# A squared-ReLU MLP in which the left half of the down projection takes seven block products for eight

## The chip, the cores and the metric

The kernel runs on one core of a Trainium2 chip. The metric is the device time of one launch, in microseconds. A core has five engines that run their own instruction queues in order and wait for each other by semaphores: TensorE (PE, matrix products into PSUM), ScalarE (ACT), VectorE (DVE), GpSimd (POOL) and SyncE (SP). In this kernel SP issues the weight loads, POOL a few small transfers, and the transfers themselves run on the core's DMA engines. PSUM has eight banks of 128 partitions by 512 float32.

## The reference

Two layers of a decoder trunk over 256 rows of 2048 columns, all in float32. Each layer is a mixer (attention of 8 heads beside a gated short convolution, one projection before and one after) and an MLP with 8192 hidden columns:

```
for l in range(DEPTH):                       # 2
    h = _rmsnorm(x, attn_norm_g[l])
    proj = h @ w_in[l]                       # 2048 x 6144: q, k, v, gate_b, gate_c, conv_in
    ...                                      # differential attention, gated causal convolution
    x = x + concat([attn, conv]) @ w_out[l]  # 2048 x 2048
    hm = _rmsnorm(x, mlp_norm_g[l]) @ w_up[l]          # 2048 x 8192
    x = x + square(relu(hm)) @ w_down[l]               # 8192 x 2048
```

## The kernel before, in words

A float32 matrix product is made of three products of halves. Each operand is split into a high part, which is the value rounded to the type that PE reads (`float32r`), and a low part, the rest; the terms are high by high, high by low and low by high (`TERMS`). Weights are loaded by SP in tiles of 512 KB (`raw`, four buffers), and each tile is split by ACT (high, L307) and DVE (low, L308) into one of three buffers, 128 by 1024 each.

There are two forms of product. `linear` (L322 to L339) holds activations still and streams 512 columns of weights: for each 128 rows of weights and each half of the 256 rows of x it issues three matmuls of 512 columns into a tile of two PSUM banks. It is used for q, k, v, o and the down projection (`dn`). `linear_t` (L341 to L364) holds 128 by 128 of weights still and streams activations, so that the result is transposed: a matmul of 512 columns does high by high and high by low at once (both parts of the activations lie side by side), and one of 256 columns does the third term. It is used for `up` and for the convolution's inputs. The two tiles of two banks that these products alternate between are called `mm`; three more banks serve transposes and small products, and one the attention's `av`.

The MLP runs in four groups of 2048 hidden columns (L650 to L666). A group first makes eight chunks of `up`, each relu'd, squared and split into `hid` tiles in SBUF, and then four products `dn`, one for each 512 columns of the output, each added onto x by two multiply-adds of DVE with the squared row scale `r2` (L659). In the last group of layer 0 each finished 512 columns of x start a `chunk` of the next normalisation (L395 on): eight transposes on PE, four splits of 128 by 256 by ACT (L244) and DVE (L245) into the next layer's `nT`, and two sums of squares on ACT (L409).

The order on PE is that of the program as written. Attention, normalisation and other small work is written as generators that a background list advances at every `tick` between matmuls. One global `plan` lists all weight tiles of both layers in order of use, and the splits run `AHEAD` = 2 tiles ahead of the product that uses them, over all borders of stages and layers. The other engines' queues get the order that the framework's scheduler chooses. The relative bias of the attention (2 MB in SBUF) is built once at the start: two transfers of 1 MB on POOL's queue out of a small table in DRAM (L208), and eight copies on ACT (L237); it stays in SBUF for both layers.

Of the kernel before, what the change touches and what calls it, by code (L numbers as in the profile page):

```python
# [9 lines left out]
F32 = mybir.dt.float32  # L10
# [22 lines left out]
AHEAD = 2  # L33
# [65 lines left out]
def trunk(ctx: ExitStack, tc: tile.TileContext, x, w_in, w_out, conv_w, q_norm_g, k_norm_g,  # L99
# [7 lines left out]
    bpool = ctx.enter_context(tc.tile_pool(name="bpool", bufs=8))  # L107
    wpool = ctx.enter_context(tc.tile_pool(name="wpool", bufs=3))
    nat = ctx.enter_context(tc.tile_pool(name="nat", bufs=7))
    tmp = ctx.enter_context(tc.tile_pool(name="tmp", bufs=3))  # L110
# [77 lines left out]
    bias = const.tile([P, 2 * NH, S], F32, tag="bias", name="bias")  # L188
# [6 lines left out]
    def small_setup():  # L195


# [4 lines left out]
        by_dist_d = dram.tile([2 * NH, REL], F32, name="by_dist_d")  # L202
        nc.gpsimd.dma_start(by_dist_d, by_dist)
        revs = []
        for j in range(2):
            rev = bpool.tile([P, NH, S], F32, tag="b", name=f"rev{j}")
            src = by_dist_d[j * NH:(j + 1) * NH, 0:S]
            nc.gpsimd.dma_start(  # L208
                rev, bass.AP(src.tensor, src.offset, [[1, P], [REL, NH], [1, S]]))
            revs.append(rev)  # L210
# [22 lines left out]

        yield 4
# [25 lines left out]

    def straight(w, row0, nk, col):
        return [(w, row0 + 2 * P * i, col, 2) for i in range(nk // 2)]

    def turned(w, col):
        return [(w, 4 * P * i, col, 4) for i in range(D // P // 4)]

    plan = []
    for l in range(DEPTH):  # L270
        for half in range(2):
            for part in range(3):
                plan += straight(w_in[l], 0, D // P, part * AW + half * CH)
        for q in range(AW // WC):
            for part in (4, 5):
                plan += turned(w_in[l], part * AW + q * WC)
        for q in range(AW // WC):
            plan += turned(w_in[l], 3 * AW + q * WC)
        for n in range(D // CH):
            plan += straight(w_out[l], 0, D // P, n * CH)  # L280
        for g in range(DFF // D):
            for c in range(D // WC):
                plan += turned(w_up[l], g * D + c * WC)
            for n in range(D // CH):
                plan += straight(w_down[l], g * D, D // P, n * CH)
    loaded, parts_of = [], []

    def load_weights():
        i = len(loaded)
        if i < len(plan):  # L290
            w, row, c, nk = plan[i]
            cols = 2 * CH // nk
            raw = wpool.tile([P, nk, cols], F32, tag="raw", name=f"raw{i}", bufs=RAW)
            nc.sync.dma_start(
                raw, w[row:row + nk * P, c:c + cols].rearrange("(k p) c -> p k c", p=P))
            loaded.append(raw)

    def split_weights():
        i = len(parts_of)
        if i < len(plan):  # L300
            while len(loaded) <= i:
                load_weights()
            nk = plan[i][3]
            hi = wpool.tile([P, nk, 2 * CH // nk], F32R, tag="hi", name=f"whi{i}")
            lo = wpool.tile([P, nk, 2 * CH // nk], F32R, tag="lo", name=f"wlo{i}")
            for c in (slice(0, 1), slice(1, nk)) if i < 2 else (slice(0, nk),):
                nc.scalar.activation(hi[:, c], loaded[i][:, c], AF.Copy)  # L307
                nc.vector.tensor_sub(lo[:, c], loaded[i][:, c], hi[:, c].bitcast(F32))  # L308
            parts_of.append((hi, lo))

    used = [0]

    def weights(w, row, c):

        i = used[0]
        used[0] += 1
        assert plan[i][1:3] == (row, c)
        while len(parts_of) < min(len(plan), i + 1 + AHEAD):
            split_weights()
        return parts_of[i]  # L320

    def linear(name, acts, w, row0, col0):  # L322

        acc = mm.tile([P, NT, CH], F32, tag="mm2", name=name)
        nk = len(acts) * KG
        for kp in range(nk // 2):
            hi, lo = weights(w, row0 + kp * 2 * P, col0)
            for j in range(2):
                k = kp * 2 + j
                a = acts[k // KG]  # L330
                while not a.ready:
                    work.tick()
                for t in range(NT):
                    for n, (pa, pw) in enumerate(TERMS):
                        nc.tensor.matmul(  # L335
                            acc[:, t], a.ap[:, pa, k % KG, t * P:(t + 1) * P], (hi, lo)[pw][:, j],
                            start=(k == 0 and n == 0), stop=(k == nk - 1 and n == 2))
                work.tick()
        return acc  # L339

    def linear_t(name, acts, w, col0):  # L341
# [6 lines left out]
        for k0 in range(0, nk, 4):  # L348
            hi, lo = weights(w, k0 * P, col0)
# [32 lines left out]
    class Norm:  # L382
# [31 lines left out]
        def factors(self):  # L414
# [8 lines left out]
            if self.which:  # L423
                self.r2 = small.tile([P, NT], F32, tag="rowf2", name="rowf2", bufs=2)
                nc.vector.tensor_mul(self.r2, self.r, self.r)
# [47 lines left out]
    def attention(l, qT, kT, v, h0, dst):  # L473
# [111 lines left out]
    def hidden(acc, dst, j, name):  # L585

        a = joined(acc, name)
        sq = nat.tile([P, 2, S], F32, tag="wide", name=f"{name}s")
        nc.scalar.activation(a, a, AF.Relu)
        nc.scalar.activation(sq, a, AF.Square)  # L590
        in_parts(dst, j, sq)


    norm = Norm(0, 0)
    work.start(norm.chunk(0, 0))
    for n in range(1, D // CH):
        load_weights()
        load_weights()
        load_x(n)
        work.start(norm.chunk(n, 2), 4 * n - 3)  # L600
    work.start(small_setup(), 10)

    for l in range(DEPTH):
        hT = norm.tiles
        cat = [Parts(bpool, "b", f"cat{l}{i}") for i in range(4)]
        work.start(norm.factors(), 1)
        for half in range(2):
            h0 = 4 * half
            c0 = half * CH
            acc = linear(f"q{l}{half}", hT, w_in[l], 0, c0)  # L610
            r = norm.r
            qT = bpool.tile([P, 2, 4, S], F32R, tag="b", name=f"qT{l}{half}")
            work.start(qk_norm(acc, r, qT, q_gain[:, l:l + 1], f"q{l}{half}"))
            acc = linear(f"k{l}{half}", hT, w_in[l], 0, AW + c0)
            kT = bpool.tile([P, 2, 4, S], F32R, tag="b", name=f"kT{l}{half}")
            work.start(qk_norm(acc, r, kT, k_gain[:, l:l + 1], f"k{l}{half}"))
            acc = linear(f"v{l}{half}", hT, w_in[l], 0, 2 * AW + c0)
            v = bpool.tile([P, 2, NT, CH], F32R, tag="b", name=f"v{l}{half}")
            for t in range(NT):
                nc.scalar.activation(v[:, 0, t], acc[:, t], AF.Copy, scale=r[:, t:t + 1])  # L620
                nc.vector.scalar_tensor_tensor(v[:, 1, t], acc[:, t], r[:, t:t + 1],
                                               v[:, 0, t].bitcast(F32),
                                               op0=ALU.mult, op1=ALU.subtract)
            work.start(attention(l, qT, kT, v, h0, cat[half]), 3)
        cv = bpool.tile([P, AW // P, S], F32, tag="b", name=f"cv{l}")
        for q in range(AW // WC):
            acc = linear_t(f"gc{l}{q}", hT, w_in[l], 4 * AW + q * WC)
            u = joined(acc, f"gc{l}{q}")
            nc.gpsimd.tensor_tensor(u, u, norm.bc(2), op=ALU.mult)
            acc = linear_t(f"ci{l}{q}", hT, w_in[l], 5 * AW + q * WC)  # L630
            i = joined(acc, f"ci{l}{q}")
            nc.vector.tensor_mul(u, i, u)
            conv(l, q, u, cv, norm)
        for q in range(AW // WC):
            acc = linear_t(f"gb{l}{q}", hT, w_in[l], 3 * AW + q * WC)
            gate(q, acc, cv, cat[2 + q // 2])

        norm = Norm(1, l)
        for n in range(D // CH):
            acc = linear(f"o{l}{n}", cat, w_out[l], 0, n * CH)  # L640
            for t in range(NT):
                nc.vector.tensor_add(xs[n][:, t], acc[:, t], xs[n][:, t])
            work.start(norm.chunk(n, 2))

        mT = norm.tiles
        G = D // CH
        last = l == DEPTH - 1
        mnorm, norm = norm, None if last else Norm(0, l + 1)
        work.start(mnorm.factors(), 1)
        for g in range(DFF // (G * CH)):  # L650
            hid = [Parts(bpool, "b", f"hid{l}{g}{c}") for c in range(G)]
            for c in range(2 * G):
                acc = linear_t(f"up{l}{g}{c}", mT, w_up[l], g * D + c * WC)
                hidden(acc, hid[c // 2], c % 2, f"h{l}{g}{c}")
            final = g == DFF // (G * CH) - 1
# [42 lines left out]
```

## Time and profile before

| | |
|---|---|
| three runs, median (lowest to highest) | 2207.14 us (2206.47 to 2209.34) |
| the profiled execution, its own time | 2209.4 us |
| its span | 2207.6 us |
| mean granted clock of PE | 0.999 |
| busy: PE, DVE, ACT, POOL | 2193.6, 1257.4, 1105.3, 100.3 us |
| moved by DMA | 410.99 MB, mean 186 GB/s |
| the MLPs in the chain, start to end | 405.9 to 1112.5 and 1499.0 to 2202.9 us |

The span is the time between the first and the last instruction of the profile; the execution's own time has 1.8 us more around it. A row of the groups view gives line, engine, operation, output and inputs, shape and count, then the busy time and the mean of one in ns, then the engine's idle time before such instructions with what ended it. A row of the windows view gives the stretch, the busy time of PE, weight load, DVE, ACT and POOL with the number of instructions, then the granted clock, the DMA engines' busy share and the bytes moved. In the chain, a piece is start, duration, what ran, and how many instructions.

### The profile page before, as it was taken

The numbers are of one execution on the slowest core, as the hardware profiler recorded it, in microseconds if no ns is written. First come the engines' busy times: TensorE is split into PE (matmuls) and PEld (weight loads), VectorE is DVE, ScalarE is ACT, GpSimd is POOL, SyncE is SP. The second block draws the span as 40 slices with busy tenths as digits, with TensorE's granted clock in tenths as the row PEclk, the third lists the DMA queues.
The fourth block names the chain that finished last, engine by engine and source line by source line (L and its number), as shares of the span: only waits on it lengthen the run. The fifth ranks groups of instructions, "written<-read, shape, count | busy, mean of one in ns | idle before, by whom it ended". The sixth has DMA issues, their size and how long they took to land.

```text
span 2207.6 us, 28973 instructions
## 1 busy us (share of the span) xinstructions
PE 2193.6 (99%) x11242; PEld 1863.1 (84%) x11242; DVE 1257.4 (57%) x1561; ACT 1105.3 (50%) x1492; POOL 100.3 (5%) x120
## 2 busy tenths in 40 slices
PE   8999999999999999999999999999999999999999
PEld 6888888888888888888888888888888888888887
DVE  5577655555555555555556776555555555555554
ACT  6456445554454454355445664445534544544543
POOL 3021100000000000000011211000000000000000
PEclk9999999999999999999999999999999999999999
DMA  7554666666666666666666546666666666666665
GB/s 250 172 158 148 191 183 189 187 187 191 197 186 188 199 187 186 194 194 184 186 185 179 156 153 187 186 185 189 188 191 196 187 190 197 185 189 199 186 197 162
DMA packets 302698, 410.99 MB, mean 186 GB/s; under 512 B 12931, under 2 KB 193749, under 8 KB 302560
## 3 DMA queue, kind: packets, MB, share of 16 engines
q1 hardware_dynamic: 301520, 406.90, 61.0%
q0 software_dynamic: 992, 2.22, 0.3%
q8 instruction: 88, 1.44, 0.3%
q14 instruction: 50, 0.41, 0.1%
q10 hardware_dynamic: 48, 0.02, 0.0%
HBM read 406.96 MB, written 2.12 MB: 185 GB/s over the span
## 4 chain that ended last, share of the span: by engine, by line
PE 99%; DMA 0%; POOL 0%; DVE 0%; ACT 0%; issue 0%; SPq 0%; DVEq 0%
PE up L357 32%; PE dn L335 32%; PE o L335 8%; PE q L335 4%; PE gc L357 4%; PE ci L357 4%; PE gb L357 4%; PE k L335 4%; PE v L335 4%; PE sc L487 1%; PE av L523 1%; PE tpn L399 1%; DMA raw<-in_w_in_dram 0%; PE ptp L513 0%; PE atp L549 0%; POOL q_r L379 0%
## 5 line engine op out<-in xcount | busy, mean ns | idle before, releaser
L308 DVE TENSOR_TENSOR wlo<-raw,whi 128x1024 fp32r<-128x1024 f32 (+1 forms) x770 | 944.0, 1226 | 835.1 <-ACT whi L307 831.5
L307 ACT ACTIVATE whi<-raw 128x1024 fp32r<-128x1024 f32 (+1 forms) x770 | 813.3, 1056 | 991.9 <-PE dn L335 387.8
L335 PE MATMUL dn<-whi,hid 128*128 128x512 f32 x2048 | 632.7, 389 | 0.0
L357 PE MATMUL up<-nT,whi 128*128 128x512 f32 x2048 | 512.6, 392 | 0.0
L335 PEld LDWEIGHTS dn<-whi,hid 128*128 128x128 f32 x2048 | 384.4, 188 | 79.6
L357 PEld LDWEIGHTS up<-nT,whi 128*128 128x128 f32 x2048 | 368.8, 189 | 66.3
L335 PE MATMUL dn<-wlo,hid 128*128 128x512 f32 x1024 | 398.5, 389 | 0.0
L357 PEld LDWEIGHTS up<-nT,wlo 128*128 128x128 f32 x2048 | 279.3, 190 | 19.8
L357 PE MATMUL up<-nT,wlo 128*128 128x256 f32 x2048 | 285.7, 282 | 0.0
L335 PEld LDWEIGHTS dn<-wlo,hid 128*128 128x128 f32 x1024 | 192.2, 188 | 39.5
L335 PE MATMUL o<-whi,cat 128*128 128x512 f32 x512 | 159.6, 390 | 0.0
L335 PEld LDWEIGHTS o<-whi,cat 128*128 128x128 f32 x512 | 96.1, 188 | 19.8
L335 PE MATMUL o<-wlo,cat 128*128 128x512 f32 x256 | 99.6, 389 | 0.0
L335 PE MATMUL q<-whi,nT 128*128 128x512 f32 x256 | 86.0, 405 | 2.8 <-ACT nT L244 2.8
L335 PE MATMUL k<-whi,nT 128*128 128x512 f32 x256 | 86.6, 405 | 0.0
L335 PE MATMUL v<-whi,nT 128*128 128x512 f32 x256 | 83.4, 396 | 0.0
L357 PE MATMUL gc<-nT,whi 128*128 128x512 f32 x256 | 65.8, 396 | 0.0
L357 PE MATMUL ci<-nT,whi 128*128 128x512 f32 x256 | 65.3, 396 | 0.0
L357 PE MATMUL gb<-nT,whi 128*128 128x512 f32 x256 | 64.1, 392 | 0.0
L335 PEld LDWEIGHTS q<-whi,nT 128*128 128x128 f32 x256 | 48.9, 191 | 14.6 <-ACT nT L244 3.2
L335 PEld LDWEIGHTS k<-whi,nT 128*128 128x128 f32 x256 | 48.9, 191 | 11.0
L335 PEld LDWEIGHTS o<-wlo,cat 128*128 128x128 f32 x256 | 48.1, 188 | 9.7
(645 smaller groups left out, 1580.5 us busy)
## 6 DMA issues: line engine op xcount, KB each, us to landing
raw<-in_w_up_dram SPq DMA_DIRECT2D x256, 512.0 KB, 3.7
raw<-in_w_down_dram SPq DMA_DIRECT2D x256, 512.0 KB, 3.7
raw<-in_w_in_dram SPq DMA_DIRECT2D x192, 512.0 KB, 4.0
raw<-in_w_out_dram SPq DMA_DIRECT2D x64, 512.0 KB, 3.7
rev<-by_dist_d POOLq DMA_DIRECT2D x2, 1024.0 KB, 11.6
out_dram<-x SPq DMA_DIRECT2D x8, 256.0 KB, 3.9
x<-in_x_dram SPq DMA_DIRECT2D x3, 512.0 KB, 9.5
x<-in_x_dram SPq DMA_DIRECT2D x2, 256.0 KB, 3.8
```

Of the source, the lines that this page charges most:

```text
L307: nc.scalar.activation(hi[:, c], loaded[i][:, c], AF.Copy)
L308: nc.vector.tensor_sub(lo[:, c], loaded[i][:, c], hi[:, c].bitcast(F32))
L335: nc.tensor.matmul(acc[:, t], a.ap[:, pa, k % KG, t * P:(t + 1) * P], (hi, lo)[pw][:, j], start=(k == 0 and n == 0), stop=(k == nk - 1 and ...
L357: nc.tensor.matmul(acc[:, f, 0] if part else acc[:, f], wt[:, k % 4, fs], a.ap[:, 0, k % KG] if part else a.ap[:, :, k % KG], start=(part ...
L399: nc.tensor.transpose(tp[:, i * S + t * P:i * S + (t + 1) * P], xs[n][:, t, k * P:(k + 1) * P], ident)
L487: nc.tensor.matmul(sc[:, :W], qT[m * DK:(m + 1) * DK, a, i, t * P:(t + 1) * P], kT[m * DK:(m + 1) * DK, b, i, :W], start=(n == 0), stop=(n ...
L523: nc.tensor.matmul(av[:, i * P:(i + 1) * P], pT[:, a, k * P:(k + 1) * P], v[:, b, k, i * P:(i + 1) * P], start=(k == 0 and n == 0), stop=( ...
```

## The change

The left 1024 of the 2048 output columns of the down projection are computed with seven block products for eight. Blocks are: two neighbouring runs of 128 hidden rows (a *pair* of hidden blocks, 32 pairs per layer), two halves of 128 rows of x, and two halves of 512 output columns. For each pair the weights need four sums (t1 to t4) and the activations four sums (S1 to S4), and the seven products of all 32 pairs stay in seven PSUM banks until the end of the stage, where eleven operations of DVE and one of ACT combine them onto x (L854 to L872 of the new file). The eighth bank takes the up columns.

The new `mlp` (L666) therefore runs by pairs. In each of 32 steps two `up_column`s of 128 hidden columns (32 matmuls each, L767) alternate with the 21 matmuls of the pair two steps earlier (`LAG`). `evict` (L788) copies the bank by ACT and adds the two halves by DVE. `square` (L793) does relu, a factor for the upper half of the rows, square, sends the hidden values to DRAM by POOL (256 KB), makes S1 to S4 on DVE and splits all eight blocks into `f`. `quarters` (L711) makes the weight forms: b1 and b2 are split directly from the loaded 1 MB tile `draw`; t1 and t3 come from a copy times minus one on ACT (L724) onto which a transfer of POOL's queue adds 512 KB of w_down out of DRAM (L725); t2 and t4 are an add and a subtract on DVE. When all pairs are through, the right 1024 columns run as before with 24 matmuls per pair, with the hidden values loaded back from DRAM (L886) and split again.

Round this: every stage has its own `Weights` list, so that splits no longer run ahead over a border; `AHEAD` is 3; the mixer's bias, temporary and raw-weight pools and `bpool` are opened inside `mixer` (L598 on) and the MLP's pools inside `mlp`, over the same SBUF; the bias is built anew for the second layer (`load_bias`, L226); the rows' scale is folded into a factor on half of the rows and one scale at the end. In layer 0 the next normalisation's chunks 0 and 1 start after the combining and chunks 2 and 3 after the last product.

```diff
-AHEAD = 2
+AHEAD = 3
+NP = DFF // (2 * P)
+LAG = 2
...
+            def parts(src, tag, bufs):
+                hi = spool.tile(list(src.shape), F32R, tag=f"{tag}h", name=f"{tag}h", bufs=bufs)
+                lo = spool.tile(list(src.shape), F32R, tag=f"{tag}l", name=f"{tag}l", bufs=bufs)
+                nc.scalar.activation(hi, src, AF.Copy)
+                nc.vector.tensor_sub(lo, src, hi.bitcast(F32))
+                return hi, lo
+            def quarters(i):
+                def plain():
+                    raw = forms["raw"] = load_rows(i, 0).rearrange("p k (n c) -> p k n c", n=2)
+                    h1, l1 = parts(raw[:, 0, 0], "b1", 2)
+                    h2, l2 = parts(raw[:, 1], "b2", 1)
+                    return (h1, l1), (h2[:, 0], l2[:, 0]), (h2[:, 1], l2[:, 1])
+                def sums():
+                    raw = forms["raw"]
+                    t = forms["t"] = spool.tile([P, 4, CH], F32, tag="t", name="t", bufs=2)
+                    nc.scalar.activation(t[:, 0:2], raw[:, 0], AF.Copy, scale=-1.0)
+                    nc.gpsimd.dma_start(
+                        t[:, 0:2], w_down[l][i * 2 * P:(i + 1) * 2 * P, CH:2 * CH].rearrange(
+                            "(k p) c -> p k c", p=P), accum_op=ALU.add)
+                    h, lw = parts(t[:, 0:2], "t13", 1)
+                    nc.vector.tensor_add(t[:, 2], t[:, 1], raw[:, 0, 0])
+                    nc.vector.tensor_sub(t[:, 3], raw[:, 1, 0], t[:, 2])
+                    return (h[:, 0], lw[:, 0]), (h[:, 1], lw[:, 1])
...
+            for i in range(NP + LAG):
+                j = i - LAG
+                if i < NP:
+                    h = fpool.tile([P, 8, P], F32, tag="h", name="h", bufs=1)
+                    evict(up_column(f"up{l}{i}a", i < LAG),
+                          h[:, 0:2].rearrange("p a c -> p (a c)"))
...
+                if j >= 0:
+                    b11, b21, b22 = weights.take()
+                    t1, t3 = weights.take()
+                    product(0, j, A11, b11)
+                    product(1, j, A12, b21)
+                    product(2, j, S4, b22)
+                    product(4, j, S1, t1)
+                if i < NP:
+                    evict(up_column(f"up{l}{i}b", i < LAG),
+                          h[:, 2:4].rearrange("p a c -> p (a c)"))
+                    fs[i] = square(i, h)
+                if j >= 0:
+                    t2, t4 = weights.take()
+                    product(6, j, S3, t3)
+                    product(5, j, S2, t2)
+                    product(3, j, A22, t4)
+            e1 = wide("e1")
+            nc.scalar.activation(e1, p1, AF.Copy, scale=mnorm.scale)
+            onto(xs[0][:, 0], p2, xs[0][:, 0])
...
+            for i in range(NP):
+                back = nat.tile([P, 2, S], F32, tag="wide", name="back")
+                nc.sync.dma_start(back.rearrange("p k s -> p (k s)"), hid[i])
+                f = fpool.tile([P, 2, 2, S], F32R, tag="f", name="fr")
+                nc.scalar.activation(f[:, 0], back, AF.Copy)
+                nc.vector.tensor_sub(f[:, 1], back, f[:, 0].bitcast(F32))
```

More of the change, by code (lines that the diff above doesn't have):

```diff
@@ L232, in small_setup, with load_bias @@
         nc.vector.tensor_copy(nlam, lps[:, :DEPTH])
+    def load_bias(l, bpool, bias):
+        if l == 0:
+            yield from small_setup()
+        revs = []
+        for j in range(2):
+            rev = bpool.tile([P, NH, S], F32, tag="b", name=f"rev{l}{j}")
+            src = by_dist_d[j * NH:(j + 1) * NH, 0:S]
+            nc.gpsimd.dma_start(
+                rev, bass.AP(src.tensor, src.offset, [[1, P], [REL, NH], [1, S]]))
+            revs.append(rev)
         yield 4
@@ L603, in trunk @@
[L603 to L655, printed above, removed]
-            for n in range(D // CH):
-                acc = linear(f"dn{l}{g}{n}", hid, w_down[l], g * G * CH, n * CH)
-                for t in range(NT):
-                    nc.vector.scalar_tensor_tensor(
-                        xs[n][:, t], acc[:, t], mnorm.r2[:, t:t + 1], xs[n][:, t],
-                        op0=ALU.mult, op1=ALU.add)
-                    if final and last:
@@ L663, in trunk @@
                         nc.sync.dma_start(
                             out[0, t * P:(t + 1) * P, n * CH:(n + 1) * CH], xs[n][:, t])
-                if final and not last:
-                    work.start(norm.chunk(n, 2))
+            else:
+                work.start(norm.chunk(0, 2), 12)
+                work.start(norm.chunk(1, 2), 24)
+            acc = [mm.tile([P, NT, CH], F32, tag="mm2", name=f"dn{l}{n}") for n in range(2)]
+            for i in range(NP):
+                back = nat.tile([P, 2, S], F32, tag="wide", name="back")
[3 more added lines that the diff above has]
+                nc.vector.tensor_sub(f[:, 1], back, f[:, 0].bitcast(F32))
+                for k in range(2):
+                    b = weights.take()
+                    for n in range(2):
+                        for t in range(NT):
+                            for m, (pa, pw) in enumerate(TERMS):
+                                nc.tensor.matmul(
+                                    acc[n][:, t], f[:, pa, k, t * P:(t + 1) * P], b[pw][:, n],
+                                    start=(i == 0 and k == 0 and m == 0),
+                                    stop=(i == NP - 1 and k == 1 and m == 2))
+                        work.tick()
@@ new lines, in mlp, with first_loads @@
+            for n in range(2):
+                for t in range(NT):
+                    onto(xs[2 + n][:, t], acc[n][:, t], xs[2 + n][:, t])
+                    if last:
+                        nc.sync.dma_start(
+                            out[0, t * P:(t + 1) * P, (2 + n) * CH:(3 + n) * CH],
+                            xs[2 + n][:, t])
+                if not last:
+                    work.start(norm.chunk(2 + n, 2))
+        return norm
+    norm = Norm(0, 0)
+    def first_loads(weights):
+        for n in range(1, D // CH):
+            weights.load_early(2)
+            load_x(n)
+            work.start(norm.chunk(n, 2), 4 * n - 3)
@@ L667, in trunk @@
+    work.start(norm.chunk(0, 0))
+    for l in range(DEPTH):
+        mnorm = mixer(l, norm, first_loads if l == 0 else lambda weights: None)
+        norm = mlp(l, mnorm, l == DEPTH - 1)
     work.finish()
```

329 lines of the change are left out of this document (247 added, 82 removed).

## The prediction

> **What bounds the kernel now.** I read the busy table and the slices first, then the chain that ended last, then the stage windows, then the groups by line, the transfers and the one early stall. The page:
>
> ```profile
> PE 2193.6 (99%) x11242; PEld 1863.1 (84%) x11242; DVE 1257.4 (57%) x1561; ACT 1105.3 (50%) x1492; POOL 100.3 (5%) x120
> PEclk9999999999999999999999999999999999999999
> ```
>
> The chain, two of its pieces, and the windows of the same two stages (a group of up, a group of dn; after the busy times come PEclk, DMA share, GB/s):
>
> ```profile
> 580.51 89.36 PE up L357 x512
> 669.87 87.07 PE dn L335 x384
> ...
> 580.51:669.87 89.36, 89.36 (x513) 78.66 (x513) 49.57 (x48) 50.03 (x61) 0.00 (x0) 1.00 0.63 189
> 669.87:756.93 87.06, 87.06 (x385) 72.07 (x385) 44.42 (x40) 35.31 (x36) 0.00 (x0) 1.00 0.63 193
> ```
>
> PE never waits: the MLP is matmuls end to end at full clock, DVE is busy for 55% and 51% of the stages, the DMA engines for 63%. So any matmul removed is time, as long as nothing else comes late. One dn matmul (512 columns) takes 87.07/384 = 0.2267 us. An up group is half such matmuls, half of 256 columns: (89.36 - 256 x 0.2267)/256 = 0.1223 us.
>
> **What is removed.** Seven products for eight on the left half is 21 matmuls in place of 24 for each of 32 pairs of 128 hidden rows, in 2 layers: 192 x 0.2267 = **43.5 us**, 0.68 us per pair. The up product and the right half keep their matmuls. A pair of up and left half lasts 32 up matmuls (5.585 us) twice and 21 x 0.2267 = 4.76: 15.93 us for 16.61 before.
>
> **What the other engines carry per pair.** Prices:
>
> ```profile
> L307 ACT ACTIVATE whi<-raw 128x1024 fp32r<-128x1024 f32 x766 | 811.0, 1059 | 986.7 <-PE dn L335 387.8 <-PE up L357 302.2 <-PE o L335 83.5
> L369 ACT ACTIVATE gb0l<-gb 128x512 f32<-128x512 f32 x2 | 1.2, 586 | 0.0
> L409 ACT ACTIVATE junk<-x 128x512 f32<-128x512 f32 x32 | 19.7, 617 | 0.0
> ```
>
> ```profile
> L308 DVE TENSOR_TENSOR wlo<-raw,whi 128x1024 fp32r<-128x1024 f32 x766 | 941.5, 1229 | 830.9 <-ACT whi L307 827.3 <-PE up L357 2.4
> L659 DVE SCALAR_TENSOR_TENSOR x<-dn,rowf,x 128x512 f32<-128x512 f32 x64 | 45.1, 747 | 18.3 <-PE dn L335 18.3
> L642 DVE TENSOR_TENSOR x<-o,x 128x512 f32<-128x512 f32 x16 | 10.3, 686 | 3.2 <-PE o L335 3.2
> L516 DVE TENSOR_TENSOR pT<-ptp,pT 128x256 fp32r<-128x256 f32 x16 | 6.7, 417 | 0.2
> L516 DVE TENSOR_TENSOR pT<-ptp,pT 128x128 fp32r<-128x128 f32 x16 | 4.5, 279 | 0.0
> ```
>
> ACT: nine 1024s (four up splits, b2, t copy, t13, t24, f), three 512s (b1, relu, square), two evictions: 9 x 1.059 + 3 x 0.617 + 2 x 0.586 = 12.6 us of 15.93. DVE: eight 1024s, three 512s (b1, two for t2 and t4), three 256s, four 128s: 8 x 1.229 + 3 x 0.686 + 3 x 0.417 + 4 x 0.279 = 14.3 us, 90%. Both fit, DVE barely; rows of single instructions count their overlap twice, so this is its upper end. The before kernel's cover (half of DVE idle) is mostly spent.
>
> **The steady pairs.** The tight place is the single bank of the up columns. Column b's first matmul may start after column a (5.585) and twelve product matmuls (2.72), 8.30 us into the pair. ACT's queue ahead of that bank's eviction is the next column's split (from 5.6), the f copy, then the eviction. The rows below show a 1024 free ACT 0.97 us after its start, so the eviction ends at 5.6 + 0.97 + 0.97 + 0.59 = 8.13. It holds, by 0.17 us; I take 0 and keep 0.1 to 0.3 us in 60 pairs (6 to 18 us) as a rival.
>
> ```profile
> 1112.54 1.06 ACT L307 ACTIVATE whi<-raw 128x1024 fp32r<-128x1024 f32 x1 [1.66 <-PE dn L335]
> ...
> 1113.51 0.61 ACT L409 ACTIVATE junk<-x 128x512 f32<-128x512 f32 x1
> ```
>
> The accumulating transfer (512 KB on POOL's queue, behind the 256 KB store of the hidden rows) has no row. From its issue, t's add on DVE and the t13 split are due some 7.8 us later, and PE itself 8.7. Nearest rows:
>
> ```profile
> raw<-in_w_up_dram SPq DMA_DIRECT2D x256, 512.0 KB, 3.7
> rev<-by_dist_d POOLq DMA_DIRECT2D x2, 1024.0 KB, 11.6
> out_dram<-x SPq DMA_DIRECT2D x8, 256.0 KB, 3.9
> ```
>
> ```profile
> 29.29 1.81 POOL L208 DMA_DIRECT2D rev<-by_dist_d  x2 [1.66 <-DMA by_dist_d<-by_dist]
> ```
>
> A plain 512 KB load plus POOL's issue is 3.7 + 0.9 = 4.6 us; the 1 MB POOL transfer took 11.6. I take 6.5, nearer the load, the same bytes in long rows: free. At 11.6 it costs 2.9 us in each of 60 pairs, 174 us. Bytes: 2 MB of up, 1 of down, 0.5 accumulated, 0.25 stored per pair is 3.93e6 bytes / 15.93 us = 247 GB/s (280 if the accumulate reads its destination), against a peak of
>
> ```profile
> 10.00:12.00 2.00, 2.00 (x7) 1.52 (x6) 2.00 (x6) 2.00 (x7) 0.95 (x2) 1.00 1.05 397
> 35.00:40.00 5.00, 5.00 (x24) 4.12 (x23) 3.06 (x7) 2.92 (x4) 0.97 (x3) 1.00 1.01 355
> ```
>
> which it fits. The Trainium skill's "DMA: Bandwidth & Descriptors", section "Anatomy of one DMA — SWDGE (gpsimd) path", gives 2.0 us + bytes/436e3 for a POOL transfer, an estimate of 3.2 us here; its "Rules for kernel authors" say that an accumulate reads its destination and writes it later, so one might count the bytes twice, 4.4 us; no run here shows either, and by both the steady pairs stay free as in my sum. They speak against the slow-transfer rival; the 11.6 us row speaks for it.
>
> **The serial places.** The old kernel crossed every stage with weights already split. After this change each stage has pools of its own over the same memory, and the queues drain. Going through each engine's order by hand, with the rows above:
>
> (a) Start of each MLP. The first 1 MB of w_down overlays a pool that the last o matmul still reads, so it is issued only after that; 3.7 us for 512 KB and another 512 KB at some 370 GB/s is 5.1 us. The b1 split of it stands in ACT's queue ahead of the second half of the last normalised chunk, which PE needs for its first column. PE waits about 4.2 us (3 to 6). Twice: 8.4. The first pairs' ramp: 0.5.
>
> (b) Drain of the last two pairs. After the last up column PE has 30 matmuls (6.8 us) before it needs f(31). In front of f(31) on ACT stand: eviction, t13, two right-half splits, relu, t24, b2 (6.5 us to here), then t13, square, t24 and one more right-half split, whose 1 MB load reuses the buffer that b2's low half (1.2) frees: 6.5 + 1.2 + 5.1 = 12.8, split and f copy 2 x 1.06, low half 1.23: about 16.2 against 6.8. Late 9.5 us (7 to 11). Twice: 19. The load is issued from SP in order; behind it wait the next right-half loads, which nobody needs yet.
>
> (c) Combining. After the last product DVE does six multiply-adds and three adds before the first right-half f can get its low half: 6 x 0.747 + 3 x 0.686 = 6.5, less the overlap back to back; PE waits 5.5 (4.5 to 7). Twice: 11. The reload of hidden rows behind it is covered by this. Before, the 64 multiply-adds stood beside matmuls.
>
> (d) Layer boundary. The next layer's q waits for the banks that the last multiply-adds read, and chunks 2 and 3, started together, need four transposing banks of three, whose splits stand behind a weight split. Before, the chunks came one dn product apart, and the same place shows no wait:
>
> ```profile
> 1112.51 2.73 PE q L335 x12
> 1115.23 0.88 PE tpn L399 x8
> 1116.11 6.84 PE q L335 x30
> ```
>
> 1.0 + 3.5 = 4.5 us (1 to 7). Second reload of the bias: eight ACT copies late, 1.5 (0 to 3). The end of the kernel and the right half itself: 0 (24 matmuls = 5.44 us per pair against 1.31e6 bytes, 241 GB/s, and three splits).
>
> (e) The clock. The only real stall of the old trace, and what followed:
>
> ```profile
> 50.65 0.40 PE L335 MATMUL k<-whi,nT 128*128 128x512 f32 x1
> 53.41 0.66 PE L465 MATMUL q00tp<-ident,q00n 128*128 128x128 f32 x4 [2.37 <-DVE q00n L456]
> ```
>
> ```profile
> 54.00:55.00 1.00, 1.00 (x5) 0.82 (x4) 1.00 (x2) 0.69 (x1) 0.00 (x0) 0.72 0.29 104
> 55.00:56.00 1.00, 1.00 (x3) 0.73 (x3) 0.81 (x2) 0.00 (x0) 0.00 (x0) 0.50 0.46 63
> 56.00:57.00 1.00, 1.00 (x4) 0.80 (x3) 0.00 (x0) 0.75 (x1) 0.00 (x0) 0.50 0.79 260
> 57.00:58.00 1.00, 1.00 (x4) 0.79 (x3) 0.66 (x1) 0.31 (x1) 0.00 (x0) 0.57 0.53 203
> 58.00:60.00 2.00, 2.00 (x10) 1.62 (x9) 0.56 (x1) 0.16 (x1) 0.00 (x0) 1.00 0.26 26
> ```
>
> 2.37 us without work cost 0.28 + 0.50 + 0.50 + 0.43 = 1.7 us of clock afterwards. Seven stalls above that length: 12 us (4 to 16). The Trainium skill, "TensorE: Matmul & The Clock Gate", Part 1, says that the rate halves after an idle window of about 3.4 us and comes back after as long a busy one. The trace agrees with the way back (0.50 for some 3.3 us) and not with the threshold, since 2.37 us sufficed. By the page, (d)'s two short waits and those of (a) in part would be spared, some 5 us less in the sum.
>
> **Sum.** 8.4 + 0.5 + 19 + 11 + 4.5 + 1.5 + 12 = 57 us of cost (34 to 75 by the ends) against 43.5 saved: +13.4 us on the profiled execution's 2209.4, which lies 2.3 above the median of 2207.14; so 2222.8, or about **2220 us** in the terms of the median, slower by 0.6%. By the ends alone 2198 to 2239.
>
> **Rivals.**
> 1. The gain is kept. The stages' matmuls go and the serial places cost 10 to 20 us: for this the drain's f(31) must come in time, so that (b) falls from 19 to a few us. For it: PE 99% of a chain with nothing else in it. Against it: the order in ACT's queue. 2207 - 43.5 + 10 to 25: 2172 to 2190. It decides where the waits together stay below 43.5 us.
> 2. The accumulating transfer is too slow. Price (L - 8.7) x 60: 10 us gives +78, 2300; 11.6 gives 2395. Decides from L = 8.7. For it the rev row, against it the 512 KB rows.
> 3. The bank's 0.17 us doesn't hold, or DVE at 90% becomes the bound: 0.1 to 0.3 us each pair, 2226 to 2240, up to 2260 with long waits.
> 4. The clock stays up in the stalls, (e) falls away: 2208, next to no change. For it: nothing in this trace; against it: the 0.50 rows after a stall shorter than most of these.
>
> **Chances.** Forecast with its own range 2198 to 2239: 0.50; rival 1: 0.20; rival 2: 0.13; rival 3: 0.12; rival 4: 0.05. A measurement of this kernel tells about 0.2% (4.4 us) from no change. Faster: rival 1 and the forecast's low end, 0.24; within: 0.13; slower: 0.63. The range 2185 to 2285 leaves out most of rival 1 and of rival 2.
>
> **What would show it.** Right: in the new trace PE busy falls by about 43 us, the steady pairs are 15.9 us with no idle PE, and the idle of PE stands at six places, behind f(31), behind fr's low half, behind the first b1 split's load, and at the second layer's first q. Accumulating transfers land within 7.8 us. Wrong: PE idle spread evenly over the pairs (rival 2 if DVE waits for the transfer, rival 3 if PE waits for the eviction), or six places of 1 us (rival 1).

## The result

| | median of the runs (lowest to highest) |
|---|---|
| the kernel before | 2208.24 us (2206.47 to 2209.40) |
| the changed kernel | 2422.47 us (2413.23 to 2425.18) |
| ratio | 1.0962, 95% interval 1.0937 to 1.0986 |

The changed kernel is 9.6% slower; the prediction said 0.6% slower (2220 us) and gave 2185 to 2285 as its range. The direction was right and the size was not: the time lies 202 us above the forecast and 137 us above the top of the range.

The page of the changed kernel, busy times and the rows of its slices for the clock (span 2418.2 us):

```profile
PE 2240.0 (93%) x11054; PEld 1875.2 (78%) x11054; DVE 1556.7 (64%) x2239; ACT 1340.5 (55%) x1822; POOL 209.7 (9%) x250
PEclk9999999999999999899999999999999999998999
...
uraw<-in_w_up_dram SPq DMA_DIRECT2D x128, 1024.0 KB, 6.9
draw<-in_w_down_dram SPq DMA_DIRECT2D x128, 1024.0 KB, 5.5
t<-in_w_down_dram POOLq DMA_DIRECT2D x64, 512.0 KB, 10.7
```

PE has fewer matmuls (11054 for 11242) and is yet busy for longer: its mean granted clock is 0.962, where it was 0.999. It is idle for 178 us where it was idle for 14. The accumulating transfer takes 10.7 us to land (the median of 64). Who waits for it stands in the view of waits (waiting instruction, what it waited for, total us, times, longest):

```profile
DVE t L730 <- DMA t<-in_w_down_dram: 345.8, 62, 8.2
ACT h L797 <- DVE h L791: 233.7, 55, 6.7
```

One pair in the trace, first DVE's queue, then POOL's issue of the transfer it waits for, then ACT's queue behind DVE, then PE in this pair and its two neighbours (start, duration, instruction, idle time before it):

```profile
709.37 1.22 DVE L708 TENSOR_TENSOR b2l<-draw,b2h 128x1024 fp32r<-128x1024 f32 x1
717.90 0.69 DVE L730 TENSOR_TENSOR t<-t,draw 128x512 f32<-128x512 f32 x1 [7.31 <-DMA t<-in_w_down_dram]
718.51 1.22 DVE L693 TENSOR_TENSOR ulo<-uraw,uhi 128x1024 fp32r<-128x1024 f32 x1
...
721.39 0.42 DVE L791 TENSOR_TENSOR h<-ev 128x256 f32<-128x256 f32 x1
```

```profile
705.47 1.20 POOL L725 DMA_DIRECT2D t<-in_w_down_dram  x1 [1.32 <-ACT t L724]
```

```profile
721.84 0.63 ACT L797 ACTIVATE h<-h 128x512 f32<-128x512 f32 x1 [6.53 <-DVE h L791]
...
727.68 0.58 ACT L790 ACTIVATE ev<-up017a 128x512 f32<-128x512 f32 x1
```

```profile
688.19 3.78 PE L779 MATMUL up015b<-nT,uhi 128*128 128x512 f32 x8 [4.00 <-ACT ev L790]
710.56 2.00 PE L779 MATMUL up016b<-nT,uhi 128*128 128x512 f32 x8
728.31 3.78 PE L779 MATMUL up017b<-nT,uhi 128*128 128x512 f32 x8 [4.42 <-ACT ev L790]
```

The transfer is issued at 705.47, and the add that waits for it starts at 717.90, 12.4 us later. This reader, the add for t2, is the next thing in DVE's queue at 710.6, five microseconds after the issue. Behind the add stand the up weights' low halves and the sum of the evicted column, so relu, square, S1 to S4 and the split into f come late, ACT's queue comes late behind them, and with it the eviction of the one bank that the up columns share. PE waits there (52 waits for this eviction in the timeline, 120 us in all, up to 4.7 us each). In the rows shown it then runs at about half rate: eight matmuls of 512 columns take 3.78 us after such a wait and 2.00 without. After 29 of the 52 waits the first eight take 2.58 us or more.

The sum itself is not needed so early. Counted in order from the start of the layer, the transfer issued at 705.47 and the add at 717.90 are the 17th of their kind, and the 17th splits of t1 and t3 and of t2 and t4 on ACT are these:

```profile
737.48 1.06 ACT L707 ACTIVATE t13h<-t 128x1024 fp32r<-128x1024 f32 x1
...
741.34 1.05 ACT L707 ACTIVATE t24h<-t 128x1024 fp32r<-128x1024 f32 x1
```

So the scheduler has put the copy, the transfer and the add a whole pair ahead of the splits (t has two buffers): the split of t1 and t3 comes 32 us after the issue, and that of t2 and t4 23 us after the add. DVE stands still for sums that are split only a pair later.

### The profile page after: what moved, and what is told of

Its sections match the earlier page's. It is cut to its first block, busy times and chain, and to the rows that moved or that the text cites. A ratio compares the mean times of both kernels' runs of the same rounds, so it can differ in the third digit from the quotient of the medians.

```text
span 2418.2 us, 29438 instructions
## 1 busy us (share of the span) xinstructions
PE 2240.0 (93%) x11054; PEld 1875.2 (78%) x11054; DVE 1556.7 (64%) x2239; ACT 1340.5 (55%) x1822; POOL 209.7 (9%) x250
## 4 chain that ended last, share of the span: by engine, by line
PE 49%; issue 39%; DMA 5%; POOL 4%; DVE 2%; ACT 2%; POOLq 0%; SPq 0%; DVEq 0%; ACTq 0%
PE dn L895 15%; PE o L337 7%; PE gc L359 4%; PE ci L359 4%; PE q L337 4%; PE gb L359 4%; PE v L337 4%; PE k L337 3%; DMA t<-in_w_down_dram 3%; POOL t L725 3%; PE pr L818 1%; POOL hid L802 1%; DMA draw<-in_w_down_dram 1%; DMA hid<-h 1%; PE sc L499 1%
## 5 line engine op out<-in xcount | busy, mean ns | idle before, releaser
L282 DVE TENSOR_TENSOR wlo<-raw,whi 128x1024 fp32r<-128x1024 f32 (+1 forms) x258 | 317.3, 1231 | 242.8 <-ACT whi L281 241.5
L281 ACT ACTIVATE whi<-raw 128x1024 fp32r<-128x1024 f32 (+1 forms) x258 | 271.3, 1053 | 310.6 <-PE o L337 73.6
L692 ACT ACTIVATE uhi<-uraw 128x1024 fp32r<-128x1024 f32 x256 | 269.4, 1052 | 219.1 <-PE o L337 10.0
L693 DVE TENSOR_TENSOR ulo<-uraw,uhi 128x1024 fp32r<-128x1024 f32 x256 | 312.2, 1221 | 29.3 <-ACT uhi L692 25.4
L895 PE MATMUL dn<-whi,fr 128*128 128x512 f32 x1024 | 320.3, 393 | 9.8 <-ACT fr L888 8.1
L282 DVE TENSOR_TENSOR wlo<-draw,whi 128x1024 fp32r<-128x1024 f32 x128 | 156.7, 1226 | 155.0 <-ACT whi L281 155.0
L895 PEld LDWEIGHTS dn<-whi,fr 128*128 128x128 f32 x1024 | 194.4, 190 | 51.8 <-ACT fr L888 8.9
L281 ACT ACTIVATE whi<-draw 128x1024 fp32r<-128x1024 f32 x128 | 135.6, 1061 | 178.2 <-PE dn L895 171.1
L895 PE MATMUL dn<-wlo,fr 128*128 128x512 f32 x512 | 200.9, 392 | 0.0
L818 PE MATMUL pr<-t13h,f 128*128 128x512 f32 x256 | 100.3, 394 | 0.0
L725 POOL DMA_DIRECT2D t<-in_w_down_dram x64 | 77.1, 1205 | 138.2 <-ACT t L724 136.0
## 6 DMA issues: line engine op xcount, KB each, us to landing
t<-in_w_down_dram POOLq DMA_DIRECT2D x64, 512.0 KB, 10.7
```

The costliest lines, as they stand in the source:

```text
L281: nc.scalar.activation(hi[:, k], raw[:, k], AF.Copy)
L282: nc.vector.tensor_sub(lo[:, k], raw[:, k], hi[:, k].bitcast(F32))
L692: nc.scalar.activation(hi, src, AF.Copy)
L693: nc.vector.tensor_sub(lo, src, hi.bitcast(F32))
L725: nc.gpsimd.dma_start(t[:, 0:2], w_down[l][i * 2 * P:(i + 1) * 2 * P, CH:2 * CH].rearrange("(k p) c -> p k c", p=P), accum_op=ALU.add)
L818: nc.tensor.matmul(prods[n], f[:, pa, a], b[pw], start=(i == 0 and m == 0), stop=(i == NP - 1 and m == 2))
```

## The experiments

Every time is the median of the runs beside the kernel before on the same chip (2208.1 to 2209.1 us); the intervals are of the ratio to it.

**e1 and e2: the transfer without the add.**

```diff
-nc.gpsimd.dma_start(t[:, 0:2], w_down[...], accum_op=ALU.add)
+nc.gpsimd.dma_start(t[:, 0:2], w_down[...])      # e1
+nc.sync.dma_start(t[:, 0:2], w_down[...])        # e2
```

> The transfer of 512 KB onto t is issued from POOL at the same place, after the same copy, but overwrites t instead of being added to it (the sum is left out, so t1 to t4 are not the sums they should be). In the changed kernel it took 10.7 us to land, and 62 of 64 times DVE waited for it, 345.8 us in all. Theory A, that adding in flight is what makes it slow: it lands in 4.6 to 6.5 us, DVE's wait falls under 60 us, the kernel takes 2422 - 200 = about 2220 us. Theory B, that any transfer of POOL's queue is slow beside the 1 MB loads: still 9 us or more, about 2420 us. Theory C, that the pairs are long for another reason (DVE's load, the one bank of the up columns): the transfer lands early and the time still stays above 2350 us.

> The same plain transfer (sum left out), issued from SP. Theory A: as e1, about 2220 us. Theory B: 4 to 5.5 us to land where e1 had 9 or more, about 2220 us, and e1 stays at 2420. If SP's queue is in the way (the transfer waits for t's copy on ACT, and the next up and down loads stand behind it), the loads come later and PE waits at the splits: 2230 to 2300 us under both.

e1 took 2221.63 us (1.0043 to 1.0073), e2 2219.13 (1.0033 to 1.0066). In e1's page, then e2's:

```profile
t<-in_w_down_dram POOLq DMA_DIRECT2D x64, 512.0 KB, 7.1
```

```profile
t<-in_w_down_dram SPq DMA_DIRECT2D x64, 512.0 KB, 5.1
```

The same bytes at the same place in the program take 10.7 us added, 7.1 us plain from POOL and 5.1 us plain from SP. Theory A had 4.6 to 6.5 us and under 60 us of DVE's waiting for e1; it is 7.1 us, and DVE still waits 78.7 us in all, but PE no longer waits in the steady pairs. So theory A holds in the main: without the add the transfer is early enough, and what lay above some 2220 us is gone. Theory B falls with e1.

**e3 and e4: the sum without a transfer.** The loaded 1 MB tile holds all four operands of t1 and t3.

```diff
-nc.scalar.activation(t[:, 0:2], raw[:, 0], AF.Copy, scale=-1.0)
-nc.gpsimd.dma_start(t[:, 0:2], w_down[...], accum_op=ALU.add)
+nc.vector.tensor_sub(t[:, 0:2], raw[:, :, 1], raw[:, 0])                          # e3
+nc.gpsimd.tensor_tensor(t[:, 0:2], raw[:, :, 1], raw[:, 0], op=ALU.subtract)      # e4
```

> The sum t1, t3 is made by one subtraction of DVE, 128x1024, from the loaded tile, which holds all four operands; ACT's copy and the transfer are gone, the result is the same. DVE's work is 14.3 + 1.2 = 15.5 us by single durations, some 13.9 us with the overlap of back to back instructions, for a pair of 15.93. Theory A and B: pairs of 15.9 to 16.2 us, 2422 - 200 = 2210 to 2235 us, with the serial places of the prediction left (measured in the changed kernel as 3.7, 6.7, 5.8 and 3.0 us). Theory C: DVE is the bound, pairs of 16.6 us and more, above 2260 us.

> The same subtraction on POOL, which stands idle: 128x512 took 2.24 us there, so 128x1024 is 4.5 us, within the 7.8 us that the transfer had. Theory A and B: 2200 to 2230 us, at or a little below e3 as DVE is spared 1.2 us a pair. If POOL's and DVE's accesses slow each other, DVE's 1024s rise above 1.3 us while POOL works and the pairs are longer than e3's: 2240 to 2300 us.

e3 took 2218.62 us (1.0028 to 1.0058). Its long window over the pairs, and one period of the eviction's sum:

```profile
460.00:900.00 440.00, 440.00 (x2348) 380.51 (x2347) 392.63 (x527) 301.92 (x361) 15.12 (x28) 1.00 0.67 210
```

```profile
652.78 0.42 DVE L788 TENSOR_TENSOR h<-ev 128x256 f32<-128x256 f32 x1
...
668.71 0.42 DVE L788 TENSOR_TENSOR h<-ev 128x256 f32<-128x256 f32 x1
```

PE is busy for 440 of 440 us at full clock, DVE for 89%, and the period is 15.93 us, the number of the prediction. Theory C falls. e4 took 2254.03 us (1.019 to 1.0221), longer than e3 although DVE has less to do; its pairs last 16.43 us:

```profile
648.91 2.54 DVE L801 TENSOR_TENSOR h<-h 128x128 f32<-128x128 f32 x1
```

```profile
648.89 2.40 POOL L724 TENSOR_TENSOR t<-draw 128x1024 f32<-128x1024 f32 x1
```

POOL needs only 2.4 us for the subtraction, and the DVE add of 128x128 that starts beside it takes 2.54 us in place of 0.29, pair after pair (mean 2307 ns over 64). DVE is held for as long as POOL's instruction runs, and ACT's split into f waits for DVE behind it (76.0 us in 59 waits). The time is in the range that the expectation gave for engines that slow each other, but not by its sign: DVE's 1024s stay at 1.21 to 1.23 us. The Trainium skill, "SBUF — State Buffer", section "SBUF: two separate sides", says that the two engines share a pair of ports as an exclusive lock, held for a whole instruction, which a DVE operation with two inputs in SBUF takes against a POOL operation that reads SBUF; these rows agree.

**e5: the add later in DVE's queue.** The transfer stays; its reader is ordered behind the low half of the pair before's t2 and t4. (`behind` gives the scheduler an order between two instructions of one engine.)

```diff
-nc.vector.tensor_add(t[:, 2], t[:, 1], raw[:, 0, 0])
+ins = nc.vector.tensor_add(t[:, 2], t[:, 1], raw[:, 0, 0])
+if "t24" in marks:
+    behind(ins, marks["t24"])
```

> The accumulating transfer stays as it is; only DVE's queue is changed: the add onto t that waits for it (and holds everything behind it on DVE) is put behind the low half of the pair before's t2, t4, about half a pair later, 12 us behind the transfer's issue in place of 5. Theory A1, that the transfer is slow but early enough, and the harm is where its reader stands in an in-order queue: DVE's wait falls from 345.8 to under 80 us, pairs of 15.9 to 16.5 us, 2215 to 2245 us in all. Theory A2, that the transfer's slowness itself (its traffic, its descriptors) is in the way of the other work: DVE waits as long as before or the loads come later, and the time stays above 2350 us.

e5 took 2219.41 us (1.0038 to 1.0068), 203 us less than the changed kernel, with the same work, the same transfer and one instruction moved.

```profile
643.30 1.20 POOL L733 DMA_DIRECT2D t<-in_w_down_dram  x1 [1.33 <-ACT t L732]
```

```profile
657.57 0.68 DVE L738 TENSOR_TENSOR t<-t,draw 128x512 f32<-128x512 f32 x1
```

```profile
460.00:900.00 440.00, 440.00 (x2351) 380.47 (x2350) 365.38 (x499) 330.75 (x387) 49.67 (x56) 1.00 0.86 243
```

The add now stands 14.3 us behind the issue, and the transfer (9.7 us to landing here) is in time; DVE's wait for it is 4.6 us in all. PE is busy throughout. So theory A1 holds and A2 falls: it was the transfer's length together with the place of its reader in an in-order queue. e1 takes away the one and e5 the other, and either is enough.

The same window of e1 shows the same traffic, 243 GB/s, so the two compare the transfer with and without the add: 9.7 and 7.1 us.

```profile
460.00:900.00 440.00, 440.00 (x2348) 380.12 (x2348) 363.65 (x502) 327.22 (x389) 35.69 (x56) 1.00 0.77 243
```

**e6, e7, e8: the serial places mended by order.** Seven edits of order at the places that the prediction named; none removes work. e7 has one more: the first two subtractions for t stand behind the last chunk's splits on DVE. The core of it, shortened, with comments in place of some of the code:

```diff
+# start: first pair's weight splits behind the last chunk's splits (ACT);
+#        halves of the first two columns in the order a0 b0 a1 b1
+if marks["pair"] == 0:
+    behind(ins, marks["gained"])
+# drain: the last pair's t splits and the right half's first splits behind f(31)
+behind(ins, marks["f"])
+# combining: first reload and its split ahead of it; the next layer's loads behind
+#        the last reload; the last pair (k, n) in the order 00 10 01 11; chunk 3 later
+first = reload(0)
...
-work.start(norm.chunk(2 + n, 2))
+work.start(norm.chunk(2 + n, 2 + 4 * n))
```

> The changed kernel with its early add, and the serial places mended by order alone: the first pair's weight splits behind the last chunk's splits, the first two columns' halves interleaved, the splits of t and of the right half behind the last f on ACT, the first hidden tile's reload and split ahead of the combining, the next layer's first loads behind the last reload, the last pair's right half by halves of the columns, chunk 3 four ticks after chunk 2. If the serial places cost what e3's idle shows (36 us of waits and some 12 of clock, six places) and are independent of the steady pairs: 2422 - (30 to 48) = 2374 to 2392 us. If they are hidden behind the slow pairs: above 2405.

> e3 (t1, t3 by one subtraction of DVE) with the same mended places. By the prediction's sum, what e3 lacks of the 43.5 us is the serial places: 2218.6 - (30 to 48) = 2170 to 2189 us, faster than the kernel before by 0.9 to 1.8%. If something else takes the gain (clock, DVE at its limit): above 2200.

> The accumulating transfer kept, the add placed later as in e5, and the serial places mended as in e6: e5's time less 30 to 48 us, 2170 to 2200 us. If so, the change as such was sound and two orders in queues made it slower; if it stays above 2209, the transfer costs more than its wait.

e6 (on the changed kernel) took 2384.02 us (1.0788 to 1.0820): 38 less. e7 (on e3) took 2203.99 us (0.9971 to 0.9990): 15 less. e8 (on e5) took 2198.64 us (0.9946 to 0.9975): 21 less. All three were expected to gain 30 to 48 us, and only e6 does; e7 ends 15 us above its range, and e8 at the upper end of the 2170 to 2200 us that were written down for it. In e7 and e8 much of the cost stays, because the wait moves: e8's PE still waits 3.22 us before the first product and 2.17 us at f(31). e6 gains 20.5 us of PE's idle time, as e8 does against e5 (16.5), and another 16 us of busy time. What the clock costs can be summed from the windows view, by steps of 1 us, as busy time times what the granted clock lacks of 1. In 1100 us of the pairs (550 us in each layer) that is 57 us in the changed kernel and 56 in e6; outside them it falls from 19 to 2 us. So e6's extra gain is clock at the serial places, not in the pairs.

**e9 to e11: one place at a time, on e5.**

> e5 with the start of each MLP mended alone (first weight splits behind the last chunk's, the first two columns' halves interleaved). e5 waits 0.98 + 3.69 + 1.71 and 0.98 + 3.71 + 0.92 us there; e8, with the same mending, still 1.71 + 0.48 + 3.22 and as much again, now before the first product. So the wait moves more than it goes: 1 to 6 us, 2213 to 2219 us. If the start's wait is all gained: 12 us and 3 of clock, 2204.

> e5 with the drain alone mended (the last pair's t splits and the right half's first splits behind f(31) on ACT). e5's waits there are 1.14 + 5.80 and 1.14 + 5.92 us, e8's 2.17 + 0.53 twice: 8.6 us less and 0 to 3.4 of clock: 2207 to 2211 us. The prediction's 9.5 us per layer would give 19: 2200.

> e5 with the combining and the layer's border alone mended (first reload and split ahead of the combining, next layer's loads behind the last reload, the last pair by halves of the columns, chunk 3 later). e5 waits 5.75, 2.49 + 1.45, 1.10 + 2.98 us there, e8 some 5 in all: 9 us less and 2 to 5 of clock: 2205 to 2209 us.

e9 took 2223.53 us (1.0050 to 1.0078), 4 more than e5; e10 2212.96 (1.0007 to 1.0025), 6 less; e11 2202.54 (0.9959 to 0.9981), 17 less. Together 19, where e8 had 21. None of the three lies in its expected range: e9 is 4.5 us above, e10 2 above, e11 2.5 below. The start's mending is a loss. PE's timeline in e9, then ACT's and DVE's in front of the first f:

```profile
407.01 0.46 PE L443 MATMUL rbc<-diag,ones 128*128 128x128 f32 x2 [1.71 <-DVE nT L256]
...
435.66 0.77 PE L846 MATMUL pr<-b1h,f 128*128 128x512 f32 x1 [3.30 <-issue]
```

```profile
430.94 1.06 ACT L736 ACTIVATE t<-draw 128x1024 f32<-128x1024 f32 x1 [1.70 <-DMA draw<-in_w_down_dram]
...
434.50 1.06 ACT L836 ACTIVATE f<-h 128x1024 fp32r<-128x1024 f32 x1
```

```profile
432.98 1.23 DVE L701 TENSOR_TENSOR ulo<-uraw,uhi 128x1024 fp32r<-128x1024 f32 x1 [1.68 <-ACT uhi L700]
434.12 0.28 DVE L834 TENSOR_TENSOR h<-h 128x128 f32<-128x128 f32 x1
```

The two waits of e5 at the first column (0.98 and 3.69 us) are gone; one of 1.71 us stands in their place, and the first f is late. The load of the third w_down tile is issued at 423.91, where e5 had 419.59; ACT's copy out of it waits for it, and splits of up weights, DVE's last sum S4 and f stand behind it. PE is idle for as long as in e5 (51.7 and 52.0 us) and busy for 5 us more. e10's moves on as well: f(31) is waited for 2.17 + 0.53 us instead of 1.14 + 5.80, but the first right-half matmul 8.56 instead of 5.75, since its splits now stand behind f. In e11 the border's waits are gone and only e5's start and drain are left.

**e12: three more orders.**

```diff
+if i == 2: behind(ins, marks["f0"])                      # pair 2's copy to t, ACT
+if marks["pair"] == NP - 1 and tag == "b2": behind(marks[tag], marks["S4"])
+if i == NP - 1: behind(ins, marks["S4"])                 # the last pair's add onto t
-behind(ins, marks["f"])
+behind(ins, marks["hi t24"])                             # right half's first splits
-yield 5
+yield 10                                                 # product that spreads the rows' ratio
```

> e8 with three more orders: the third pair's copy to t behind the first f on ACT, the last pair's b2 low half, t sums and right-half splits behind S4 and t2, t4 of the last pair, the product that spreads the rows' ratio five ticks later. They are meant for e8's waits of 1.71, 3.22 and 2.17 + 0.53 us, twice each, with some 5 us of clock: 2198.6 - (8 to 20) = 2179 to 2191 us. If they only move, as at the start in e8: 2195 to 2199.

e12 took 2193.37 us (ratio 0.9928, 0.9914 to 0.9941): 0.7% faster than the kernel before, with all of the change's work in it and the accumulating transfers too. It missed its range by 2 us. PE's idle time fell from e8's 35.5 us only to 30.5, for new waits came up: 1.65 us before the second pair's second column, 1.50 and 2.21 us at the right half's first products (layer 0).

## Why the prediction was wrong, by its own steps

**The step that failed** is "I take 6.5, nearer the load, the same bytes in long rows: free". The transfer took 10.7 us, within the prediction's bounds (4.6 to 11.6) and near the other end. For a plain POOL transfer 6.5 was a fair guess (7.1 in e1); for the adding one the load's row was no guide: 10.7 lies beside the 11.6 us of the row that moved twice the bytes. And "free" failed on DVE, not on PE: in the place of a reader due 7.8 us after the issue the runs showed one that stood 5.1 us after it, at the head of everything else in DVE's queue. The estimates of 3.2 and 4.4 us that the prediction worked out from "DMA: Bandwidth & Descriptors" of the Trainium skill (sections "Anatomy of one DMA — SWDGE (gpsimd) path" and "Rules for kernel authors"), and that spoke for the low end, lie below the medians of POOL's transfers here (7.1 plain; 10.7 added in the changed kernel, 9.7 in e5).

**The rival that came true was priced too low, and what it hit, it hit by luck.** Its formula, (10.7 - 8.7) x 60, gives 120 us. PE's idle time and busy time, from the two pages' first lines, are 178.2 and 2240.0 us in the changed kernel and 52.0 and 2165.2 in e5:

```profile
PE 2165.2 (98%) x11054; PEld 1834.3 (83%) x11054; DVE 1569.3 (71%) x2239; ACT 1362.4 (61%) x1822; POOL 208.6 (9%) x250
```

So the changed kernel has 126 us more of waiting and 75 us more of busy time. Of the 75, some 63 are clock by the sum over windows of 1 us (75.9 us in the changed kernel, 13.2 in e5, 1.7 in the kernel before), 57 of them behind the waits in the pairs; the rest stays open. The prediction priced the clock for seven stalls and not for sixty. That the formula's 120 is close to the waiting is luck. It counts from the split of t1 and t3 and PE's use of them, due 7.8 and 8.7 us after the issue, and by e5's 9.7 us it would charge 60 us where nothing was lost. In the trace that split comes 32 us after the issue, and PE waits for the bank of the up columns, at the end of a path from DVE's add over relu, f and the eviction, which the prediction didn't draw for this rival. At 0.13 the rival also had too small a chance for a duration without a row.

**What was taken as fixed and wasn't:** the 7.8 us until the add is due. The trace had 5.1 us for the add and 32 us for the split, and e5 shows that the add could stand 14.3 us behind without any loss. The walk asked whether the transfer is in time, and not whether its reader needs to stand there.

**What held.** The saving and the steady pair: 15.93 us in e3, PE 440 of 440 us in e3 and e5. The eviction's margin of 0.17 us and DVE's 83 to 89%: no wait of PE. The serial places, against e5's trace, where nothing else is in the way:

| place | predicted us | e5, layer 0 and 1 |
|---|---|---|
| (a) start | 4.2 each | 0.98 + 3.69; 0.98 + 3.71 |
| first pairs' ramp | 0.5 in all | 1.71; 0.92 |
| (b) drain | 9.5 each | 1.14 + 5.80; 1.14 + 5.92 |
| (c) combining | 5.5 each | 5.75; 2.49 + 1.45 |
| (d) layer border | 4.5 | 1.10 + 2.98 |
| bias reload | 1.5 | no wait seen |
| (e) clock | 12 | 11.5 by the windows; 15.1 of busy time |
| sum | 57 | 53.1 |

```profile
409.03 1.65 PE L789 MATMUL up00a<-nT,uhi 128*128 128x512 f32 x3 [3.69 <-DVE nT L256]
922.00 0.79 PE L828 MATMUL pr<-b1h,f 128*128 128x512 f32 x1 [5.80 <-ACT f L818]
934.65 0.80 PE L905 MATMUL dn<-whi,fr 128*128 128x512 f32 x1 [5.75 <-ACT fr L898]
1121.34 0.63 PE L409 MATMUL tpn<-ident,x 128*128 128x128 f32 x4 [2.98 <-DVE nT L256]
```

The 15.1 us are e5's busy PE, 2165.2, less 2193.6 - 43.5. Of them 11.5 are clock by the windows (13.2 less the 1.7 of the kernel before), and 3.6 stay open. The sum is the 15.1 and e5's idle 52.0 less the 14.0 of the kernel before; the waits listed are 39.8 us, and elsewhere e5 is idle for 1.8 us less. That it makes up e5's 2219 us is so by construction, and it is the single rows that bear the prediction out. e5, where the transfer costs nothing as the prediction took it, took 2219.41 us for the forecast 2220; so near a hit is luck in part, for the drain was priced too high by 5 us in all, the bias reload by 1.5, and the first pairs' ramp too low by 2. At the drain, ACT does wait for the right half's load in front of f(31), but less than the 6.3 us (b2's low half and the load) of the prediction:

```profile
918.28 1.06 ACT L289 ACTIVATE whi<-draw 128x1024 fp32r<-128x1024 f32 x1 [2.79 <-DMA draw<-in_w_down_dram]
```

The clock falls to 0.50 after a wait, as in the prediction's rows. In the changed kernel's pairs, the 19 waits for the eviction of up to 1.75 us left the first eight matmuls at full rate (2.11 to 2.14 us); of the 33 from 1.87 us on, 29 were followed by slower ones, and four, of 2.34 to 3.08 us, were not. The threshold of about 3.4 us in "TensorE: Matmul & The Clock Gate" of the Trainium skill, Part 1, is not borne out here. Length alone doesn't decide it: by windows of 0.5 us the stretches at 0.50 last 3.41 or 6.83 us in the steady pairs, and they start whole multiples of 3.41 us apart (686.24, 727.20 and 785.23 us: 12 and 17 times). Two windows hold the ends of the second of these: 0.60 means that 0.8 us of the first ran at half the clock.

```profile
727.00:728.00 1.00, 0.00 (x0) 0.00 (x0) 1.00 (x2) 1.00 (x2) 0.33 (x1) 0.60 0.36 87
734.00:735.00 1.00, 1.00 (x6) 0.80 (x5) 0.00 (x0) 0.00 (x0) 0.00 (x0) 0.98 1.09 294
```

**Rival 1** (the gain kept) was out by the same table: the serial places alone eat the 43.5 us. **Rival 3** didn't come true: its sign, PE waiting for the eviction, did appear, but at the end of rival 2's path, and in e3 and e5 the bank costs nothing. **Rival 4** (the clock stays up) is out by the same rows of the clock.

## What to carry to other kernels

Where a new transfer has no row in the old trace, don't choose within its bounds by likeness: find its reader's place in the in-order queue, count the microseconds from issue to that place, and if the upper bound is beyond them, give that case most of the chance, or move the reader. The order of the program as written doesn't give that place where a scheduler orders the queues: here it had put the add a pair ahead. Price a wait that recurs with the clock that it costs behind it; here that was 57 us on 120 in the pairs. And a saving of matmuls in a kernel whose engines run ahead over every border is spent at the new borders first: order alone there was worth 26 us of 43.5, and each place moved has to be looked at again, for a wait that is only pushed on is no gain.

## What the runs showed that was not expected

Adding in flight made a 512 KB transfer longer by 2.6 us beside the same traffic (9.7 us in e5, 7.1 in e1), and POOL's issue of it 1.20 us for 0.72. A subtraction on POOL of 128x1024 takes 2.42 us, where e4's expectation had 4.5 from a 128x512 product of 2.24 us; another 128x512 product in the kernel before takes 1.29 us (`gc00w<-gc00w,rowb`, L629), so the row taken was the slower of two. But it stops a DVE add beside it for the whole of that time. And one instruction of DVE moved by some 9 us is worth 203 us of 2422.
